# Stores of the squared tiles issued by GpSimd instead of ScalarE, and the last two tiles of each chunk emptied later

## The chip, the cores and the metric

The kernel runs on one core of a Trainium2 chip. Its metric is the device time of one execution in microseconds. A core has engines with a queue of instructions each: TensorE (PE) multiplies matrices, VectorE (DVE) and ScalarE (ACT) work on elements, GpSimd (POOL) and SyncE (SP) here mostly issue DMAs; any of ScalarE, GpSimd and SyncE can issue one. TensorE accumulates in PSUM banks of 128 x 512 numbers.

## The reference

One decoder layer, in float32, on 256 tokens of width 2048:

```
h = RMSNorm(x);  p = h @ W_in
A = dilated sliding-window attention (8 heads);  B = latent attention (8 heads)
x = x + RMSNorm(concat(A, B) @ W_out)
h = RMSNorm(x)
u = square(relu(h @ W_up))        # W_up 2048 x 8192
x = x + RMSNorm(u @ W_down)       # W_down 8192 x 2048
```

The change lies in the line that makes `u`, the up projection. Only float32 accuracy counts as right, so every weight and activation is split into a high part and a low part, and a product is formed from three: high by high, high by low, low by high.

## The kernel before, in words

**Splitting weights.** A tile of weights is loaded to `raw`; ScalarE writes the rounded copy `hi` (L314, or L318 where the norm's gain is multiplied in), and VectorE writes `lo`, the weight less `hi` (L315, L319). TensorE then runs the three products (`three`, L304). So each tile passes through ScalarE, then VectorE, then TensorE.

**The up projection** (the loop over `j`, 0 to 7) makes 1024 columns of `u`, a *chunk*, at a time, over 16 blocks of 128 rows of W_up. Four PSUM banks `acc_u` hold the chunk: 2 halves of the tokens (`b`) by 2 halves of the columns (`n`). Chunk 0 takes its blocks one by one. Chunks 1 to 7 take k6 to k10, then a *pair*, then k11 and k12, a pair, k13, a pair, k14 and k15. A pair (`seven_products`) replaces two blocks by seven smaller products of sums, in the manner of Strassen, and needs both row blocks of weights at once (`seven`): a load of 1 MB into the buffer `ab` or `ab2` (`load_two`, L379), VectorE's sums `t` (L366) and `u` (L370, L371), and four splits, of a corner of `ab`, of `b` (half of `ab`), of `u` and of `t`. GpSimd's queue issues these loads; those of chunk 7's pairs 1 and 2 and chunk 6's pair 2 are loaded as plain tiles by SyncE ("raw" in `UP_PAIRS`), and that of chunk 1's pair 0 by SyncE too. The profile shows both buffers as `ab`; the pairs of a chunk alternate between them, so the next load can be issued as soon as the splits of the pair before the last are done. Pairs are counted 0, 1, 2 in this text. Some of the seven products go to extra banks, `m`, which the previous chunk's `acc_u` have left.

**Emptying a chunk.** When a chunk's products are done, VectorE adds the pairs' combined banks to `acc_u` (L1259, four adds), and each of the four banks is emptied by `up_evac`: ScalarE's Relu with the norm's factor (L1043) and Square (L1044) make a tile `r` (three buffers, shared with the tiles `neg`), which is stored to `rkeep` in DRAM, 256 KB (L1046). Later it is read back in another layout (`turn_u`, `c<-rkeep`, L1059, issued by ScalarE), and VectorE transposes it in blocks of 32 (L1061) into `uT`. For some columns `lo_away` (chunks 1 to 5) then stores the negated rounded tile (`neg`, L1075; `ukeep`, L1077, issued by ScalarE) and adds `uT` to it by an accumulating DMA from GpSimd's queue (`ukeep<-uT`, L1087). The last chunk's squares go straight to `uT` and are stored from there (`rkeep<-uT`).

**What sets the order.** The program is recorded in one pass. `Flow` keeps a clock that each matmul advances by its estimated time; side work is written as generators that yield a delay, and at every `pump` those whose time has come write their next instructions. `up_evac` yields 2.4 (`UP_STEP`) times its `order` before its Relu, in a chunk's own order 0.6, 1.6, 2.6 and 3.6 for its four banks; chunk 0 passes other numbers. The loads and sums of a pair are written when TensorE's weights are taken up to a few tiles before it. Each engine then executes its own instructions in that order, waiting by semaphores.

Of the kernel before, what the change touches and what calls it, by code (L numbers as in the profile page):

```python
# [93 lines left out]
D_X0, D_X, D_SS, D_TAB = 8.0, 3.0, 3.0, (14.0, 20.0)  # L94
D_NORM, D_HT, D_SECOND = 4.5, 1.5, 4.0

UP_STEP = 2.4

D_BACK, D_TURN, D_NEG, D_LO, D_ADD = 12.0, 8.0, 9.0, 2.0, 26.0

# [171 lines left out]
def layer(nc, tc, io):  # L272
    flow = Flow()

    def pool(name, side, **kw):
        return tc.alloc_tile_pool(name=name, bufs=1, side=side, **kw)
# [9 lines left out]
    def bank(i, name):  # L286
        return ps.tile([P, 512], F32, tag=f"bank{i}", bufs=1, name=name)
# [5 lines left out]
    def acc_bank(name):  # L293
        return next_bank(0, 4, name)
# [152 lines left out]
    for c in range(2):  # L447
        wide_d.append([])
        for what, k in DOWN_STEPS[c]:
            if what == "k":  # L450
                ts = [weights.plan(down_weight(c, k), 1, CW)]
            else:
                q, parts_q, back = [lambda c=c, k=k, f=f: f(c, k) for f in (down_sums, down_split, down_back)]
# [4 lines left out]
    def in_order(n, apart=(0, 0)):  # L458

        f, l = apart[0], n - apart[1]  # L460
        return ([(t, b) for b in range(NB) for t in range(f)] + [(t, b) for t in range(f, l) for b in range(NB)]
                + [(t, b) for b in range(NB) for t in range(l, n)])

    def proj(aT, chs, name, order=None, need=None, bank_of=None):

        accs = [[[(bank_of or acc_bank)(f"acc_{name}_{c}_{b}_{i}") for i in range(len(ch.cuts))] for b in range(NB)]
                for c, ch in enumerate(chs)]
        order = order or [(0, t, b) for t, b in in_order(len(chs[0].tiles))]
        left = {(c, b): len(ch.tiles) for c, ch in enumerate(chs) for b in range(NB)}
        uses = {}  # L470
        for c, t, b in order:
            ch = chs[c]
            i, k0, kp = ch.tiles[t]
            ws = [weights.get(x) for x in (i if isinstance(i, list) else [i])]
            i = i if isinstance(i, list) else [i]
            if need:
                need(k0 + kp - 1, b)
            if i[0] < FINE:
                hl = [(0, 0), (1, 0)], [(0, 1)]
            else:  # L480
                hl = [(0, 0), (0, 1), (1, 0)],
            for g, passes in enumerate(hl):
                for kk in range(kp):
                    k = k0 + kk
                    for j, (o, m) in enumerate(ch.cuts):
                        wt, o = (ws[j], 0) if len(ws) > 1 else (ws[0], o)
                        for p, (x, w) in enumerate(passes):
                            mm(accs[c][b][j][:, :m], tok(aT[x], k, b), wt[w][:, kk, o:o + m],
                               k == 0 and g == 0 and p == 0,
                               k == ch.nk - 1 and g == len(hl) - 1 and p == len(passes) - 1, MM * m / 512)  # L490
                    flow.pump()
            left[c, b] -= 1
            for x in i:
                uses[x] = uses.get(x, 0) + 1
                if uses[x] == NB:
                    weights.free(x)
            if not left[c, b]:
                yield c, b, accs[c][b]
# [216 lines left out]
    for half in range(2):  # L715
        qkv = {}
        for nms in (("qk", "v") if not half else "qkv"):
            accs = [acc for _, _, acc in proj(xT, [ch_a[half, nms]], f"{nms}{half}",
                                              bank_of=at_bank if (half, nms) == (0, "v") else None)]
            for i, nm in enumerate(nms):  # L720
                if half and nm == "v":
                    flow.finish(*heads)
                if not half and nm != "v":
                    t = early.tile([P, NB + 1, 512], F32, name=f"{nm}_{half}")
                else:
                    t = pa.tile([P, NB + (nm != "v"), 512], F32, tag=nm, name=f"{nm}_{half}")
# [149 lines left out]
    for what, ch in ch_b:  # L876
        if what == "qr":
            flow.finish(q_chain)
        if what in ("qr", "v0", "v1"):
            if what == "qr":  # L880
                qr = lat.tile([P, NB, HB, RB], F32, tag="cq", name="qr")
            for _, b, acc in proj(latT["q" if what == "qr" else "kv"], [ch], what):
                if what == "qr":
                    out = qr[:, b].rearrange("p h d -> p (h d)")
                else:
                    i = 4 * int(what[1])
                    out = vB[:, b, i:i + 4, :].rearrange("p h d -> p (h d)")
# [3 lines left out]
        else:  # L891
            t, i = qT if what[0] == "q" else kT, 4 * int(what[1])
# [100 lines left out]
    for ns in ((0, 1), (2,), (3,)):  # L993
# [4 lines left out]
        for c, b, acc in proj(mixT, [ch_o[n] for n in ns], f"o{ns[0]}", order, heads_done):  # L998
            n = ns[c]
# [26 lines left out]
    def u_tile(j):  # L1026
        if j not in uT:
            if j in (0, 1, 10, 11, 12, 13):
                t2 = late["u01" if j < 2 else "ab2" if j < 12 else "ab"][:, j % 2 * CW:(j % 2 + 1) * CW]
            else:  # L1030
                tag = {"tag": "T", "bufs": 2} if j > 13 else {"tag": f"uT{j}", "bufs": 1}
                t2 = late["up"].tile([P, CW], F32, name=f"uT{j}", **tag)
            uT[j] = t2.rearrange("p (k s) -> p k s", k=4)
        return uT[j]

    def up_evac(j, b, acc, order):

        yield UP_STEP * order
        if j < GT - 2:
            r = late["up"].tile([P, 512], F32, tag="r", bufs=3, name=f"r{j}_{b}")  # L1040
        else:
            r = u_tile(j)[:, 2 * b:2 * b + 2, :].rearrange("p k s -> p (k s)")
        nc.scalar.activation(r, acc, AF.Relu, scale=rstd2[b])  # L1043
        nc.scalar.activation(r, r, AF.Square)  # L1044
        keep = dram.tile([P, 512], F32, name=f"rkeep{j}_{b}")
        nc.scalar.dma_start(out=keep.rearrange("(a t) (q c) -> (t q) a c", a=4, q=4),  # L1046
                            in_=r.rearrange("m (a c) -> m a c", a=4))
        flow.start(turn_u(j, b, keep), D_BACK + (8.0 if (j, b) == (GT - 1, NB - 1) else 0.0))

# [154 lines left out]
    evac = []  # L1204
    for j in range(FF // CW):
        at = {bn: 4 * (j % 2) + i for i, bn in enumerate(PARTS)}
        if j == 0:
            accs = {bn: acc_bank(f"acc_u0_{bn[0]}{bn[1]}") for bn in at}
            at = {bn: (turn[0] - 3 + i) % 4 for i, bn in enumerate(at)}
        else:  # L1210
            accs = {bn: bank(i, f"acc_u{j}_{bn[0]}{bn[1]}") for bn, i in at.items()}
        steps = wide_u[j]
        order = in_order(len(steps), (APART[1], 0)) if j == 0 else [(t, b) for t, (w, _, _) in enumerate(steps)
                                                                    for b in range(NB if w == "k" else 1)]
        for t, b in order:
            what, k, tiles = steps[t]
            if (j, t, b) == (0, 8, 0):
                flow.finish(*res)
                late["po"].release()
                mix.release()  # L1220
                late["up"] = pool("up", "right")
                late["st"] = late["up"].tile([P, ST], F32R, tag="st", bufs=1, name="st")
                for n in ("ab", "ab2", "c", "u01"):
                    late[n] = late["up"].tile([P, 2 * CW], F32, name=n)
                flow.start(all_sums())
            if (j, t, b) == (FF // CW - 1, 4, 0):
                weights.limit -= 1
                u_next = split_u(0, 0)
            if j == 1 and what == "w":
                flow.until(lambda: len(sums) > k)  # L1230
            if what == "k":
                w = weights.get(tiles[0])
                h_done(k, b)
                for n in range(2):
                    c = slice(n * 512, (n + 1) * 512)
                    three(accs[b, n], [tok(hT[x], k, b) for x in range(2)], [w[x][:, 0, c] for x in range(2)], t == 0, t == len(steps) - 1)
                    if j == 0 and t == len(steps) - 1:
                        evac.append(flow.start(up_evac(n, b, accs[b, n], 0.75 * (2 * b + n))))
                    flow.pump()
                if b == NB - 1:  # L1240
                    weights.free(tiles[0])
                continue

            first, last = k == 0, k == N_SEVEN[j] - 1
            if first:
                weights.ahead = W_AHEAD
                flow.finish(*evac[-4:])
                m = {n: bank(i, f"m{n}_{j}") for n, i in zip((1, 6, 7, 5), free)}
            blocks = [[tok(hT[x], 2 * k + kk, bb) for x in range(2)] for kk, bb in ((0, 0), (1, 0), (1, 1))]
            if last:  # L1250
                weights.ahead -= 1
            seven_products(tiles, (blocks, sums[k]), accs, m, first, last, last and N_SEVEN[j] > 3)
            if last:
                more = close(closing(), m)
        free = [at[bn] for bn in PARTS]
        if j:

            for bn in PARTS:
                nc.vector.tensor_tensor(out=accs[bn], in0=accs[bn], in1=more[bn], op=OP.add)  # L1259
            for o, (b, n) in enumerate(PARTS):  # L1260
                evac.append(flow.start(up_evac(2 * j + n, b, accs[b, n], o + 0.6)))
    weights.ahead = W_AHEAD
    u_last = evac[-4:]
    up = late["up"]
# [88 lines left out]
    for c in range(2):  # L1353
# [3 lines left out]
        accs = {(b, n): y[b][2 * c + n] for b, n in PARTS}  # L1357
# [118 lines left out]
```

## Time and profile before

| | before |
|---|---|
| timed, median of 3 | 1020.69 us (1020.38 to 1021.37) |
| profiled execution | 1022.37 us, span 1020.6 us |
| busy: TensorE | 1009.9 us (99%) |
| busy: VectorE | 841.5 us (82%) |
| busy: ScalarE | 624.8 us (61%) |
| busy: GpSimd | 101.3 us (10%) |
| stores of `rkeep` in the up projection | 28 from `r`, 4 from `uT`, 256 KB each |
| 1 MB loads into `ab` | 17 from GpSimd's queue |

A row of a timeline gives start, duration, engine, line, operation, the tile written and the tiles read, how many such instructions in a row, and in brackets how long the engine stood idle just before and what ended that. "ACTq" and "POOLq" are instructions of those engines' queues that issue a DMA. A row of the waits gives the total, the number of times and the longest. A row of DMA issues gives the number, the KB of each and the median time from issue to landing.

### The profile page before, as it was taken

What the parts mean: (1) busy time and instruction counts of PE and PEld (TensorE: products, weight loads), DVE (VectorE), ACT (ScalarE), POOL (GpSimd) and SP (SyncE); (2) the same over time, 40 slices, a digit from 0 to 9 for tenths busy, and PEclk for the clock granted to TensorE, in tenths of its full rate; (3) what the DMA queues carried; (4) which work ended last, traced back from release to release, by engine and by line L of the source; (5) the groups of instructions that cost most, each with busy time, mean ns of one, the idle gap of its engine ahead of it and who ended that gap; (6) DMA issues with size and microseconds to landing.
All of it is one profiled execution on the core that took longest, in us unless ns stands there. A gap on an engine that the chain in (4) does not pass through costs nothing.

```text
span 1020.6 us, 13297 instructions
## 1 busy us (share of the span) xinstructions
PE 1009.9 (99%) x4670; PEld 842.0 (83%) x4670; DVE 841.5 (82%) x1127; ACT 624.8 (61%) x824; POOL 101.3 (10%) x160
## 2 busy tenths in 40 slices
PE   9999999999999999999999999999999999999996
PEld 6888889898888788888888888888878888888885
DVE  6676747676656779998999989897999999898985
ACT  6585446555463567676666775676666665767661
POOL 0020302102101200000010100000110000211100
PEclk9999999999999999999999999999999999999999
DMA  8977759656687478778988979679989867888952
GB/s 286 367 248 269 244 167 310 220 173 194 199 320 209 174 286 260 245 258 247 293 271 279 284 215 302 190 255 339 346 271 389 292 241 257 296 305 327 368 188 82
DMA packets 109170, 267.07 MB, mean 262 GB/s; under 512 B 9520, under 2 KB 28464, under 8 KB 108464
## 3 DMA queue, kind: packets, MB, share of 16 engines
q1 hardware_dynamic: 65584, 175.14, 50.2%
q0 software_dynamic: 20144, 71.31, 21.1%
q10 hardware_dynamic: 23376, 19.78, 6.2%
q8 instruction: 36, 0.59, 0.2%
q14 instruction: 30, 0.25, 0.1%
HBM read 232.64 MB, written 33.56 MB: 261 GB/s over the span
## 4 chain that ended last, share of the span: by engine, by line
PE 89%; DVE 5%; DMA 2%; issue 2%; ACT 1%; POOL 0%; ACTq 0%; DVEq 0%; POOLq 0%; SPq 0%
PE acc_u L304 26%; PE y L304 19%; PE acc_o L304 8%; PE m L304 6%; PE acc_v L304 5%; PE md L304 5%; PE acc_qk L304 4%; PE acc_q L304 3%; PE acc_k L304 3%; PE acc_ckv L304 3%; DVE lo L315 2%; PE acc_cq L304 2%; DMA rkeep<-uT 1%; PE sc_b L304 1%; DMA raw<-in_w_in 1%
## 5 line engine op out<-in xcount | busy, mean ns | idle before, releaser
L315 DVE TENSOR_TENSOR lo<-raw,hi 128x1024 fp32r<-128x1024 f32 (+2 forms) x205 | 233.4, 1157 | 66.6 <-ACT hi L314 65.4
L314 ACT ACTIVATE hi<-raw 128x1024 fp32r<-128x1024 f32 (+2 forms) x205 | 202.5, 1005 | 75.5 <-DMA raw<-in_w_in 22.8
L304 PE MATMUL acc_u<-hi,hT_lo 128*128 128x512 f32 x386 | 150.3, 389 | 0.5 <-DVE hT_lo L315 0.5
L304 PE MATMUL acc_u<-hi,hT_hi 128*128 128x512 f32 x386 | 150.7, 390 | 0.0
L304 PE MATMUL acc_u<-lo,hT_hi 128*128 128x512 f32 x386 | 150.2, 389 | 0.0
L304 PE MATMUL y<-lo,uhi 128*128 128x512 f32 x358 | 139.4, 389 | 0.4 <-DVE lo L315 0.4
L304 PE MATMUL y<-hi,ulo 128*128 128x512 f32 x358 | 139.4, 389 | 0.1
L304 PE MATMUL y<-hi,uhi 128*128 128x512 f32 x358 | 139.3, 389 | 0.0
L318 ACT ACTIVATE hi<-raw,gcol 128x1024 fp32r<-128x1024 f32 x86 | 96.7, 1148 | 34.2 <-DMA raw<-in_w_up 13.7
L319 DVE SCALAR_TENSOR_TENSOR lo<-raw,gcol,hi 128x1024 fp32r<-128x1024 f32 x86 | 106.6, 1274 | 9.7 <-ACT hi L318 9.6
L304 PEld LDWEIGHTS acc_u<-hi,hT_lo 128*128 128x128 f32 x386 | 72.4, 188 | 16.0 <-DVE hT_lo L315 0.9
L304 PEld LDWEIGHTS acc_u<-hi,hT_hi 128*128 128x128 f32 x386 | 72.5, 188 | 14.9
L304 PEld LDWEIGHTS acc_u<-lo,hT_hi 128*128 128x128 f32 x386 | 72.5, 188 | 14.8
L304 PEld LDWEIGHTS y<-lo,uhi 128*128 128x128 f32 x358 | 67.2, 188 | 14.7 <-DVE lo L315 0.8
L304 PEld LDWEIGHTS y<-hi,ulo 128*128 128x128 f32 x358 | 67.2, 188 | 14.4 <-DVE ulo L315 0.5
L304 PEld LDWEIGHTS y<-hi,uhi 128*128 128x128 f32 x358 | 67.2, 188 | 14.0
L315 DVE TENSOR_TENSOR lo<-st_down,hi 128x1024 fp32r<-128x1024 f32 x46 | 55.0, 1219 | 0.8 <-ACT hi L314 0.8
L304 PE MATMUL acc_o<-hi,mixT_hi 128*128 128x512 f32 x128 | 51.3, 401 | 0.0
L314 ACT ACTIVATE hi<-u 128x1024 fp32r<-128x1024 f32 (+1 forms) x33 | 32.3, 980 | 30.3 <-PE y L304 12.0
L304 PE MATMUL md<-hi,s 128*128 128x512 f32 x138 | 49.9, 389 | 0.0
L304 PE MATMUL acc_o<-hi,mixT_lo 128*128 128x512 f32 x128 | 49.9, 390 | 0.0
L304 PE MATMUL acc_o<-lo,mixT_hi 128*128 128x512 f32 x128 | 49.8, 389 | 0.0
(356 smaller groups left out, 2046.4 us busy)
## 6 DMA issues: line engine op xcount, KB each, us to landing
raw<-in_w_up SPq DMA_DIRECT2D x86, 512.0 KB, 4.9
raw<-in_w_down SPq DMA_DIRECT2D x82, 512.0 KB, 6.3
raw<-in_w_in SPq DMA_DIRECT2D x55, 512.0 KB, 5.6
ab<-in_w_up POOLq DMA_DIRECT2D x17, 1024.0 KB, 6.9
raw<-in_w_out SPq DMA_DIRECT2D x32, 512.0 KB, 4.6
ab_down<-in_w_down POOLq DMA_DIRECT2D x11, 1024.0 KB, 9.3
ulo<-ukeep POOLq DMA_DIRECT2D x20, 512.0 KB, 6.3
rkeep<-r ACTq DMA_DIRECT2D x28, 256.0 KB, 3.6
```

The lines of the kernel that those rows point to most:

```text
L304: nc.tensor.matmul(out, a, b, start=start, stop=stop)
L314: nc.scalar.activation(hi, src, AF.Copy)
L315: nc.vector.tensor_tensor(out=lo, in0=src, in1=hi.bitcast(F32), op=OP.subtract)
L318: nc.scalar.activation(hi, src, AF.Copy, scale=g)
L319: nc.vector.scalar_tensor_tensor(out=lo, in0=src, scalar=g, in1=hi.bitcast(F32), op0=OP.mult, op1=OP.subtract)
```

## The change

The store of each squared tile is issued by GpSimd instead of ScalarE, all 32 of them. In chunks 1 to 7 the third and the fourth emptying are put later in the recorded order: 3.4 and 4.2 steps of 2.4 instead of 2.6 and 3.6. Chunk 0's emptying keeps its own order.

```
-UP_STEP = 2.4
+UP_STEP, EVAC = 2.4, (0.6, 1.6, 3.4, 4.2)
...
         nc.scalar.activation(r, acc, AF.Relu, scale=rstd2[b])
         nc.scalar.activation(r, r, AF.Square)
         keep = dram.tile([P, 512], F32, name=f"rkeep{j}_{b}")
-        nc.scalar.dma_start(out=keep.rearrange("(a t) (q c) -> (t q) a c", a=4, q=4),
+        nc.gpsimd.dma_start(out=keep.rearrange("(a t) (q c) -> (t q) a c", a=4, q=4),
                             in_=r.rearrange("m (a c) -> m a c", a=4))
...
             for o, (b, n) in enumerate(PARTS):
-                evac.append(flow.start(up_evac(2 * j + n, b, accs[b, n], o + 0.6)))
+                evac.append(flow.start(up_evac(2 * j + n, b, accs[b, n], EVAC[o])))
```

GpSimd's instructions around the start of chunk 5, before. `ab_3458` and `ab` are the two buffers: the first load of `ab_3458` here is chunk 5's pair 1, the `ab` after it chunk 5's pair 2, and the next `ab_3458` chunk 6's pair 0.

```order
L379 DMA ab<-in_w_up 128x2x1024
L1087 DMA ukeep_4704<-uT_4584 128x512
L379 DMA ab_3458<-in_w_up 128x2x1024
L379 DMA ab<-in_w_up 128x2x1024
L1087 DMA ukeep_5069<-uT_4949 128x512
L379 DMA ab_3458<-in_w_up 128x2x1024
```

The same place after the change:

```order
L379 DMA ab<-in_w_up 128x2x1024
L1087 DMA ukeep_4722<-uT_4584 128x512 x2
L1046 DMA rkeep_0_5099<-r_0_5096 128x4x128
L1046 DMA rkeep_0_5123<-r_0_5120 128x4x128
L1046 DMA rkeep_1_5160<-r_1_5157 128x4x128
L379 DMA ab_3458<-in_w_up 128x2x1024
L1046 DMA rkeep_1_5186<-r_1_5183 128x4x128
L379 DMA ab<-in_w_up 128x2x1024
L379 DMA ab_3458<-in_w_up 128x2x1024
```

Three of the four stores now stand ahead of the load for pair 1 and the fourth ahead of the load for pair 2. It is the same at the starts of chunks 2, 3, 4 and 6. At the start of chunk 1 all four stand ahead of pair 1's load.

ScalarE at the same place, from the split of the first pair's `u`, before (`acc_u_10` and `acc_u_11` are the third and the fourth bank of chunk 4):

```order
L314 ACTIVATE hi_5131<-u_0_5103 128x1024
L1043 ACTIVATE r_1_5144<-acc_u_10_4713,rstd_pre_3394 128x512
L1044 ACTIVATE r_1_5144<-r_1_5144 128x512
L1046 DMA rkeep_1_5147<-r_1_5144 128x4x128
L314 ACTIVATE hi_5152<-t_0_5102 128x1024
L1043 ACTIVATE r_1_5165<-acc_u_11_4714,rstd_pre_3394 128x512
L1044 ACTIVATE r_1_5165<-r_1_5165 128x512
L1046 DMA rkeep_1_5168<-r_1_5165 128x4x128
L318 ACTIVATE hi_5181<-raw_5179,gcol 128x1024
L318 ACTIVATE hi_5203<-raw_5201,gcol 128x1024
```

After:

```order
L314 ACTIVATE hi_5130<-u_0_5103 128x1024
L1077 DMA ukeep_5087<-neg_1_5128 128x512
L314 ACTIVATE hi_5147<-t_0_5102 128x1024
L1043 ACTIVATE r_1_5157<-acc_u_10_4710,rstd_pre_3394 128x512
L1044 ACTIVATE r_1_5157<-r_1_5157 128x512
L318 ACTIVATE hi_5176<-raw_5174,gcol 128x1024
L1043 ACTIVATE r_1_5183<-acc_u_11_4711,rstd_pre_3394 128x512
L1044 ACTIVATE r_1_5183<-r_1_5183 128x512
L318 ACTIVATE hi_5203<-raw_5201,gcol 128x1024
```

The split of `t` now precedes the third emptying, and the split of block k11 precedes the fourth. VectorE's instructions keep their order here but for the transposes. After the change, from the split of the first pair's `t` (`t_1` and `u_1` are the sums of pair 1, the two `raw` are k11 and k12):

```order
L315 TENSOR_TENSOR lo_5148<-t_0_5102,hi_5147 128x1024
L366 TENSOR_TENSOR t_1_5169<-ab_3458 128x1024
L370 TENSOR_TENSOR u_1_5170<-t_1_5169,ab_3458 128x512
L371 TENSOR_TENSOR u_1_5170<-u_1_5170,ab_3458 128x512
L319 SCALAR_TENSOR_TENSOR lo_5177<-raw_5174,gcol,hi_5176 128x1024
L319 SCALAR_TENSOR_TENSOR lo_5204<-raw_5201,gcol,hi_5203 128x1024
```

The sums of pair 1 stand ahead of the low parts of k11 and k12, as they did before. TensorE's and SyncE's orders are the same in both kernels.

More of the change, by code (lines that the diff above doesn't have):

```diff
@@ L95 @@
 D_NORM, D_HT, D_SECOND = 4.5, 1.5, 4.0
-UP_STEP = 2.4
+UP_STEP, EVAC = 2.4, (0.6, 1.6, 3.4, 4.2)
 D_BACK, D_TURN, D_NEG, D_LO, D_ADD = 12.0, 8.0, 9.0, 2.0, 26.0
@@ L1045, in up_evac @@
         keep = dram.tile([P, 512], F32, name=f"rkeep{j}_{b}")
-        nc.scalar.dma_start(out=keep.rearrange("(a t) (q c) -> (t q) a c", a=4, q=4),
+        nc.gpsimd.dma_start(out=keep.rearrange("(a t) (q c) -> (t q) a c", a=4, q=4),
                             in_=r.rearrange("m (a c) -> m a c", a=4))
@@ L1260, in layer @@
             for o, (b, n) in enumerate(PARTS):
-                evac.append(flow.start(up_evac(2 * j + n, b, accs[b, n], o + 0.6)))
+                evac.append(flow.start(up_evac(2 * j + n, b, accs[b, n], EVAC[o])))
     weights.ahead = W_AHEAD
```

## The prediction

> **What bounds the kernel now.** I read the page's totals first, then busy times cut into stretches of the up projection, then the waits, then each engine's timeline at a chunk boundary. The totals, and one chunk period plus the change to the down projection (columns: stretch, TensorE, weight loads, VectorE, ScalarE, GpSimd busy, granted clock, DMA share, GB/s):
>
> ```profile
> span 1020.6 us, 13297 instructions
> PE 1009.9 (99%) x4670; PEld 842.0 (83%) x4670; DVE 841.5 (82%) x1127; ACT 624.8 (61%) x824; POOL 101.3 (10%) x160
> ...
> 554.00:596.00 42.00, 42.00 (x187) 34.79 (x186) 39.35 (x45) 28.67 (x34) 4.02 (x5) 1.00 0.89 276
> 596.00:637.00 41.00, 41.00 (x183) 33.95 (x182) 38.26 (x43) 28.56 (x33) 2.50 (x3) 1.00 0.80 253
> ...
> 710.00:755.00 45.00, 44.57 (x196) 36.26 (x195) 44.31 (x57) 29.23 (x34) 5.58 (x8) 1.00 0.95 336
> ```
>
> TensorE sets the time: in the chunks it is busy in every microsecond, at clock 1.00. Relief of another engine can therefore gain only what TensorE lacks, 0.43 us in the last stretch. But VectorE is close behind: 39.35 of 42 us, 2.65 us free. ScalarE has 13 us free.
>
> How near VectorE follows, shown by the chain of waits (TensorE begins k11 of chunks 5 and 6) and by VectorE making chunk 6's low parts of k11 and k12:
>
> ```profile
> 571.38 1.36 PE m L304 x6
> 572.74 5.44 PE acc_u L304 x24
> ...
> 614.22 5.44 PE acc_u L304 x24
> ```
>
> ```profile
> 606.78 1.22 DVE L366 TENSOR_TENSOR t<-ab 128x1024 f32<-128x1024 f32 x1
> ...
> 609.37 2.47 DVE L319 SCALAR_TENSOR_TENSOR lo<-raw,gcol,hi 128x1024 fp32r<-128x1024 f32 x2
> ```
>
> The first low part is done at 609.37 + 2.47/2 = 610.6, and TensorE starts k11 at 614.2: a lead of 3.6 us. A VectorE delay beyond that reaches TensorE. Ahead of these low parts in VectorE's queue stands t<-ab, the first of pair 1's sums; it reads the 1 MB that GpSimd's queue loads. So the question is how early that load is issued. GpSimd's timeline, and its waits:
>
> ```profile
> 394.20 0.72 POOL L379 DMA_DIRECT2D ab<-in_w_up  x1 [29.81 <-DVE lo L315]
> ...
> 538.13 0.71 POOL L379 DMA_DIRECT2D ab<-in_w_up  x1 [6.16 <-DVE lo L315]
> 560.65 0.71 POOL L379 DMA_DIRECT2D ab<-in_w_up  x1 [21.80 <-DVE lo L315]
> 561.36 0.96 POOL L1087 DMA_DIRECT2D ukeep<-uT  x1
> ...
> POOL ab L379 <- DVE lo L315: 216.4, 16, 29.8
> ```
>
> GpSimd waits for free buffers and little else: its queue runs ahead. Chunk 5's pair 1 is loaded by the issue at 538.13, and VectorE reads it at 564.95 (below), 26.8 us later. The row at 561.36 also shows that an instruction behind a waiting load goes out only after it: the queue keeps its order.
>
> **The change part by part.** The edits act at the chunk boundary. VectorE there in chunk 5, from the first add of the old chunk's sums:
>
> ```profile
> 553.55 2.48 DVE L1259 TENSOR_TENSOR acc_u<-acc_u,c 128x512 f32<-128x512 f32 x4
> ...
> 561.07 1.23 DVE L315 TENSOR_TENSOR lo<-u,hi 128x1024 fp32r<-128x1024 f32 x1 [0.72 <-ACT hi L314]
> 563.81 1.23 DVE L315 TENSOR_TENSOR lo<-t,hi 128x1024 fp32r<-128x1024 f32 x1 [1.51 <-ACT hi L314]
> 564.95 1.22 DVE L366 TENSOR_TENSOR t<-ab 128x1024 f32<-128x1024 f32 x1
> ...
> 567.54 2.48 DVE L319 SCALAR_TENSOR_TENSOR lo<-raw,gcol,hi 128x1024 fp32r<-128x1024 f32 x2
> ```
>
> ScalarE there:
>
> ```profile
> 555.66 0.38 ACTq L1046 DMA_DIRECT2D rkeep<-r  x1
> ...
> 559.98 1.06 ACT L314 ACTIVATE hi<-u 128x1024 fp32r<-128x1024 f32 x1 [1.07 <-PE acc_u L304]
> 560.94 0.67 ACT L1043 ACTIVATE r<-acc_u,rstd_pre 128x512 f32<-128x512 f32 x1
> 561.64 0.63 ACT L1044 ACTIVATE r<-r 128x512 f32<-128x512 f32 x1
> ...
> 562.72 1.06 ACT L314 ACTIVATE hi<-t 128x1024 fp32r<-128x1024 f32 x1 [0.44 <-PE acc_u L304]
> 563.68 0.67 ACT L1043 ACTIVATE r<-acc_u,rstd_pre 128x512 f32<-128x512 f32 x1
> 564.38 0.63 ACT L1044 ACTIVATE r<-r 128x512 f32<-128x512 f32 x1
> ```
>
> What is taken away: 32 store issues on ScalarE at 0.38 us, 12 us over the up projection. It also moves hi<-t ahead of the third emptying, so VectorE's 1.51 us wait for it shrinks. On an engine 13 us free per chunk, ahead of an always busy TensorE, both are worth nothing, at most the 0.43 us.
>
> What is added: 32 store issues on GpSimd, each waiting for a Square of ScalarE. By order, pair 1's load now stands behind the third store of the same boundary (chunks 2 to 6), or behind all four (chunk 1). It can no longer go out 27 us early; it goes out after that Square. Chunk 7 loads pair 1 on SyncE and has no such load.
>
> The cost in chunk 5, from A = 553.55:
> 1. Third Square done. Before: 561.64 + 0.63 = A + 8.7. Now hi<-t (1.06) comes first, and three store issues (1.1) and their gaps fall away, but the third Relu cannot follow hi<-t earlier than u and the second negation allow. I place it at A + 9.4, 0.7 later; bounds A + 7.5 (everything ahead moves up by the issues saved) and A + 11.
> 2. The third store's issue on GpSimd. No row has this store there; neighbours are
>
> ```profile
> L1087 POOL DMA_DIRECT2D ukeep<-uT x8 | 7.5, 933 | 15.8 <-DVE acc_u L1259 15.8
> ...
> L974 POOL DMA_DIRECT2D xkeep<-x x8 | 4.3, 541 | 8.1 <-DVE hT_lo L315 6.9 <-DVE x L958 1.2
> ```
>
> both 256 KB. I take 0.93, as ukeep comes from the same place in the program; 0.54 is the other bound.
> 3. Landing of the 1 MB, counted from its issue. The median row of these loads, and then the fastest, the slowest, and the one at this very place of chunk 5 (issued 413.69, 572.05, 560.65; minimum, median, maximum of a single load):
>
> ```profile
> ab<-in_w_up POOLq DMA_DIRECT2D x17, 1024.0 KB, 6.9
> ...
> DMA to landing us min/median/max: 5.2/5.2/5.2
> ...
> DMA to landing us min/median/max: 8.9/8.9/8.9
> ...
> DMA to landing us min/median/max: 6.0/6.0/6.0
> ```
>
> I take 6.5: the 6.0 of this place plus 0.5 for the store's 256 KB directly ahead. Bounds 5.2 and 8.9.
> 4. So t<-ab starts at A + 9.4 + 0.9 + 6.5 + about 0.1 of wake-up = A + 17.0, against 564.95 − A = 11.4: **5.6 us late**, with VectorE idle and the low parts of k11 and k12 stuck behind it. VectorE cannot make it up: of its 2.65 us free per period, 0.72 + 1.51 lie before this sum, so 0.4 are left after it, and each such chunk adds its own 5.6. Chunks 2 to 6 (chunk 2 without the negations, which I neglect): 5 × 5.6 = 28.0.
>
> Chunk 1, where the load waits for the fourth Square:
>
> ```profile
> 396.49 0.63 ACT L1044 ACTIVATE r<-r 128x512 f32<-128x512 f32 x1
> ...
> 397.16 1.22 DVE L366 TENSOR_TENSOR t<-ab 128x1024 f32<-128x1024 f32 x1
> ```
>
> Three earlier store issues fall away, 1.1 us, of which I credit 0.9: Square done at 396.2, + 0.9 + 6.5 + 0.1 = 403.7, 6.6 late. VectorE's small gaps there give back 0.8: 5.8.
>
> VectorE is then 28.0 + 5.8 = 33.8 us late at chunk 6's k11. TensorE had 3.6 of lead, used up once: **30.2 us**. In chunk 7 the lead is smaller:
>
> ```profile
> 653.73 2.47 DVE L319 SCALAR_TENSOR_TENSOR lo<-raw,gcol,hi 128x1024 fp32r<-128x1024 f32 x2
> ...
> 655.70 5.44 PE acc_u L304 x24
> ```
>
> 655.70 − (653.73 + 1.24) = 0.7, so 2.9 more of the delay would show, but VectorE regains some 2.4 of it there (1.5 on the wait for the u part, the rest on earlier issues); +0.5. The down projection returns the 0.43 us. Sum: 30.2 + 0.5 − 0.4 = 30.3.
>
> Costs taken as nothing. The later third and fourth emptying: the first pair takes those two banks with the six m matmuls at 571.38, A + 17.8, and the fourth emptying should end by A + 12.5; the read-backs stay on ScalarE behind work already queued; if one came late, VectorE's transpose would wait, at the few microseconds a landing takes. Pair 2's load, now behind the fourth store, goes out at about A + 13 and lands by A + 22; before, VectorE read it at A + 20.4 (row below), now 5.6 later, A + 26: hidden by the stall itself. Without the stall it would be the next to be late.
>
> ```profile
> 573.94 1.22 DVE L366 TENSOR_TENSOR t<-ab 128x1024 f32<-128x1024 f32 x1
> ```
>
> The profiled execution took 1022.37 us around its 1020.6 us span, so the changed one should take 1052.7; the timed median of before lies 1.7 lower, at 1020.69, which gives 1051.0.
>
> A rule that adds to this: TensorE would stand still about 5.6 us in each chunk, and its granted clock in this trace has 1.00 throughout, with no such stop. The Trainium skill, in "TensorE: Matmul & The Clock Gate" (Part 1), says that an idle window of about 3.4 us halves the clock until as long a busy window has passed; by it each stall would cost some 1.7 us more of TensorE, an estimate from that page. As VectorE leads the pace by then, only the last would show, and the sum would be 1052.7. No row here tests it, and I leave it out.
>
> **The rivals.**
>
> *Heavier, 0.10.* The third Relu writes a buffer of which there are three, so it may also wait for the first store's landing. That store is issued at about A + 2.1, and lands 3.6 us on by ScalarE's queue, 7.3 by the nearest row of GpSimd's:
>
> ```profile
> rkeep<-r ACTq DMA_DIRECT2D x28, 256.0 KB, 3.6
> ...
> ukeep<-uT POOLq DMA_DIRECT2D x8, 256.0 KB, 7.3
> ```
>
> At 7.3 with 0.93 of issue the Relu starts at A + 10.3 instead of A + 8.1, 2.2 more per chunk in five chunks, 11; with landings of 8.9 for the loads, 2.4 × 6 = 14 more. Either gives 1062 to 1065, both 1076. Against it: ukeep<-uT reads and writes its target, these stores only write.
>
> *Lighter, 0.06.* ScalarE, freed of the issues, is at the third Square by A + 7.5, the issue takes 0.54, the landing 5.2: t<-ab at A + 13.3, 1.9 late. Six times that, less the 3.6, is 8 us: 1029.
>
> *Not slower, 0.07.* The loads are not held up by the stores, and TensorE stays full: 1020.3, with the 0.43 us regained. For it: a load issued 26.8 us ahead of its use could go out some 20 us later unnoticed. Against it: the order of GpSimd's instructions and the row at 561.36. The Trainium skill speaks for it, in "DMA: Bandwidth & Descriptors" (Issuing engines are not separate DMA queues): which engine issues a DMA saves or costs only its sequencer's time, little beside the transfer. The same page (Anatomy of one DMA) has semaphore waits happen on the issuing sequencer, before dispatch, and the trace agrees with that: 561.36 follows 560.65. By the first rule alone the time would be 1020.7.
>
> **How the numbers follow.** Forecast 0.77, heavier 0.10, lighter 0.06, not slower 0.07. The forecast's own bounds: landings of 5.2 in all six chunks take off 8 and ScalarE at its early bound 5 × 1.9 = 9.5, together 1034; landings of 8.9 add 14, 1065. The range 1034 to 1067 leaves out the two light cases and part of the heavy one, 0.18. A measurement of this kernel tells about 0.2% (2 us) from no change. Faster 0.02 and same 0.05 come from the case without delay; slower 0.93 is all the rest.
>
> **What would show it.** In the changed profile: VectorE idle 4 to 8 us before t<-ab of pair 1 in chunks 1 to 6, ended by the load of ab; TensorE idle about 1 to 3 us at k11 of chunk 1 and 5 to 6 in chunks 2 to 6, none in chunk 7; a chunk period of about 47 us instead of 41.5; GpSimd's loads released by ScalarE's Square (L1044) instead of VectorE's lo; the third store's issue near 0.9 us. I would be wrong if pair 1's loads still went out long before the Square, if VectorE stopped for less than 2 us per boundary, or if TensorE idled first at another place, such as the fourth emptying's banks or a late read-back.

## The result and the profile after

The changed kernel takes 1050.93 us (median of 4, 1050.11 to 1051.26) against 1020.58 us: a ratio of 1.0295, 95% interval 1.0279 to 1.0311, so 30 us slower. Its profiled execution took 1051.26 us, with a span of 1049.5 us, 28.9 more than before. One execution of a kernel below (two stores on GpSimd) took 5564 us against 1021 to 1024 for its other nine, and is left out of its median. The page's totals, and then busy times by chunk (columns as in the prediction):

```profile
span 1049.5 us, 13328 instructions
PE 1018.5 (97%) x4670; PEld 847.1 (81%) x4670; DVE 841.2 (80%) x1127; ACT 620.6 (59%) x824; POOL 125.7 (12%) x192
```

```profile
401.00:445.00 44.00, 44.00 (x195) 36.10 (x194) 39.07 (x43) 26.78 (x31) 4.38 (x6) 1.00 0.62 205
445.00:492.00 47.00, 42.80 (x183) 34.96 (x182) 39.07 (x43) 27.87 (x34) 5.16 (x8) 0.96 0.70 234
...
587.00:634.00 47.00, 43.38 (x184) 35.40 (x183) 39.06 (x43) 27.90 (x34) 6.99 (x10) 0.96 0.77 246
634.00:680.00 46.00, 42.24 (x179) 34.45 (x178) 39.77 (x45) 27.02 (x32) 5.63 (x7) 0.96 0.76 247
```

VectorE does about the same work per chunk as before (39.06 us), but a chunk now lasts some 47 us. TensorE has holes from chunk 2 on, and its granted clock is 0.96 there. GpSimd's timeline at the start of chunk 5, and VectorE's (the old chunk's add starts at A = 574.78):

```profile
577.15 0.79 POOL L1046 DMA_DIRECT2D rkeep<-r  x1 [22.05 <-ACT r L1044]
579.34 0.78 POOL L1046 DMA_DIRECT2D rkeep<-r  x1 [1.40 <-ACT r L1044]
584.60 0.75 POOL L1046 DMA_DIRECT2D rkeep<-r  x1 [4.48 <-ACT r L1044]
585.34 0.72 POOL L379 DMA_DIRECT2D ab<-in_w_up  x1
586.88 0.79 POOL L1046 DMA_DIRECT2D rkeep<-r  x1 [0.81 <-ACT r L1044]
```

```profile
574.78 2.49 DVE L1259 TENSOR_TENSOR acc_u<-acc_u,c 128x512 f32<-128x512 f32 x4
...
583.30 1.22 DVE L315 TENSOR_TENSOR lo<-t,hi 128x1024 fp32r<-128x1024 f32 x1
591.41 1.23 DVE L366 TENSOR_TENSOR t<-ab 128x1024 f32<-128x1024 f32 x1 [6.90 <-DMA ab<-in_w_up]
...
594.01 2.47 DVE L319 SCALAR_TENSOR_TENSOR lo<-raw,gcol,hi 128x1024 fp32r<-128x1024 f32 x2
```

The load of pair 1 follows the third store without a gap at 585.34; before the change it was issued 15 us before the add, now 10.6 us after it. VectorE stands idle for 6.90 us until it lands. The waits count six such stops, one per chunk from 1 to 6; and of TensorE, five:

```profile
DVE t L366 <- DMA ab<-in_w_up: 42.3, 6, 7.5
```

```profile
PE acc_u L304 <- DVE lo L319: 20.4, 5, 5.2
```

TensorE's timeline behind one of them (chunk 5, k11) shows where the rest went:

```profile
595.34 0.50 PE L304 MATMUL acc_u<-lo,hT_hi 128*128 128x512 f32 x1 [3.62 <-DVE lo L319]
...
596.58 0.63 PE L304 MATMUL acc_u<-hi,hT_lo 128*128 128x512 f32 x1
597.01 0.63 PE L304 MATMUL acc_u<-hi,hT_hi 128*128 128x512 f32 x1
597.43 0.63 PE L304 MATMUL acc_u<-lo,hT_hi 128*128 128x512 f32 x1
...
599.79 0.40 PE L304 MATMUL acc_u<-lo,hT_hi 128*128 128x512 f32 x1
600.02 0.39 PE L304 MATMUL acc_u<-hi,hT_lo 128*128 128x512 f32 x1
```

For 3.4 us (596.15 to 599.55) the matmuls start 0.43 us apart instead of 0.23. TensorE's busy time grew by 8.6 us (1009.9 to 1018.5) with the same 4670 matmuls: some 1.7 us behind each of the five stops. The 20.4 us of stops and these 8.6 are 29.0, the whole 28.9 of the span.

### The profile page after: what moved, and what is told of

It reads as the page before. It is cut to its first block, busy times and chain, and to the rows that moved or that the text cites. A ratio compares the mean times of both kernels' runs of the same rounds, so it can differ in the third digit from the quotient of the medians.

```text
span 1049.5 us, 13328 instructions
## 1 busy us (share of the span) xinstructions
PE 1018.5 (97%) x4670; PEld 847.1 (81%) x4670; DVE 841.2 (80%) x1127; ACT 620.6 (59%) x824; POOL 125.7 (12%) x192
## 4 chain that ended last, share of the span: by engine, by line
PE 78%; issue 9%; DVE 5%; DMA 4%; ACT 2%; POOL 1%; SPq 0%; DVEq 0%; POOLq 0%; ACTq 0%
PE y L304 25%; PE acc_u L304 13%; PE acc_o L304 8%; PE md L304 6%; PE acc_v L304 5%; PE acc_qk L304 4%; DMA ab<-in_w_up 3%; PE acc_q L304 3%; PE acc_k L304 3%; PE m L304 3%; PE acc_ckv L304 2%; DVE lo L319 2%; PE acc_cq L304 2%; PE sc_b L304 1%; POOL rkeep L1046 1%
## 5 line engine op out<-in xcount | busy, mean ns | idle before, releaser
L304 PE MATMUL acc_u<-lo,hT_hi 128*128 128x512 f32 x386 | 154.6, 400 | 20.4 <-DVE lo L319 20.4
L304 PE MATMUL acc_u<-hi,hT_lo 128*128 128x512 f32 x386 | 153.5, 398 | 0.4 <-DVE hT_lo L315 0.4
L304 PE MATMUL acc_u<-hi,hT_hi 128*128 128x512 f32 x386 | 153.5, 398 | 0.0
L304 PEld LDWEIGHTS acc_u<-hi,hT_lo 128*128 128x128 f32 x386 | 74.6, 193 | 16.6 <-DVE hT_lo L315 0.9
L366 DVE TENSOR_TENSOR t<-ab 128x1024 f32<-128x1024 f32 x18 | 22.0, 1221 | 42.3 <-DMA ab<-in_w_up 42.3
```

The source lines that it names most:

```text
L304: nc.tensor.matmul(out, a, b, start=start, stop=stop)
L366: tt(out=two[0], in0=two[1][:, 0:2, :], in1=two[1][:, 1:4:2, :], op=OP.add)
```

## The experiments

**The stores alone, and the order alone.** Each half of the change by itself.

```
e1:  EVAC = (0.6, 1.6, 2.6, 3.6)          # stores on GpSimd, old order
e2:  nc.scalar.dma_start(out=keep...)     # stores on ScalarE, new order
```

> The stores go to GpSimd, the emptying keeps its old order. All four stores of a boundary then stand ahead of pair 1's load in chunks 1 to 6. Theory (the load waits behind the last Square ahead of it in GpSimd's queue): the fourth Square should end about 1.1 us later than the third one does in the changed kernel, so the load lands about 1 us later in chunks 2 to 6: 1054 to 1058 us, a little slower than the changed kernel. Rival (the later third and fourth emptying is what costs): most of the loss is gone, under 1030 us. Rival (a store on GpSimd's queue costs as such): like the changed kernel, 1051 us.

Measured: 1055.83 us, ratio 1.0336 (1.0320 to 1.0351). As the queue's order says: four stores ahead of the load cost more than three. The later emptying is not the cause; with the stores on GpSimd it spares about 5 us. In chunk 5 of this kernel pair 1's load goes out 11.3 us after the add instead of 10.6, and takes 7.1 us to land instead of 6.0.

> The third and fourth emptying are later, the stores stay on ScalarE. Theory: TensorE stays full, no load waits: 1020 to 1021 us, and VectorE's wait of 1.5 us for the split of t is gone. Rival (the later emptying costs): some 1025 to 1050 us.

Measured: 1020.66 us, ratio 0.9995 (0.9986 to 1.0005). VectorE's wait for the split of `t` is gone in this profile, and with TensorE always busy that brings nothing.

**The loads first.** All 32 stores stay on GpSimd; a pair's load (`fetch`) is recorded eight weight tiles earlier, in one kernel for pair 1 only, in another for pairs 1 and 2.

```
-        for n, f in (*more, (0, fetch), (-late_sums, sums), ...
+        for n, f in (*more, (early, fetch), (-late_sums, sums), ...
...
e3:  early=8 if k == 1 and UP_PAIRS[j][1] != 'raw' else 0
e8:  early=8 if k and UP_PAIRS[j][k] != 'raw' else 0
```

> The changed kernel with one difference: pair 1's load is recorded eight weight tiles earlier, so that it stands ahead of all four stores in GpSimd's queue; all 32 stores stay on GpSimd, all emptyings late. Theory: the load goes out early again, VectorE does not wait for it, and the time is that of the kernel before: 1020 to 1022 us; pair 2's load, behind the fourth store, should land around 19 us after VectorE's first add and be just in time. Rival (stores on GpSimd cost as such, by their issue or their traffic): still 1030 to 1050 us.

Measured: 1027.56 us, ratio 1.0063 (1.0048 to 1.0078). Most of the loss is gone, but 6.4 us stay, more than expected. Its VectorE still waits for loads, in four chunks (two rows; line numbers are one or two higher in this kernel):

```profile
493.42 1.23 DVE L367 TENSOR_TENSOR t<-ab 128x1024 f32<-128x1024 f32 x1 [3.76 <-DMA ab<-in_w_up]
...
583.35 1.23 DVE L367 TENSOR_TENSOR t<-ab 128x1024 f32<-128x1024 f32 x1 [5.23 <-DMA ab<-in_w_up]
```

These are the sums of pair 2, whose load stands behind the fourth store. Behind the second of them TensorE comes to its one stop, of 3.77 us. GpSimd issued that load here:

```profile
571.50 0.76 POOL L1048 DMA_DIRECT2D rkeep<-r  x1 [1.53 <-ACT r L1046]
572.25 0.71 POOL L380 DMA_DIRECT2D ab<-in_w_up  x1
```

From 572.25 to 583.35 are 11.1 us; the loads for these four sums took 8.5 to 11.0 us to land, where I had counted 6 to 6.5. Whether these loads are the rest was put to a test:

> The changed kernel with the loads of pairs 1 and 2 recorded eight weight tiles earlier: pair 1's stands ahead of all four stores, pair 2's behind the second and ahead of the third. All 32 stores stay on GpSimd, all emptyings late. Theory (what the kernel with pair 1's load first still loses is pair 2's load behind the fourth store): VectorE waits for no load and the time is 1020 to 1021.5 us. Rival (stores on GpSimd's queue still cost something, as the 6 us of that kernel): 1025 to 1028 us.

Measured: 1020.72 us, ratio 0.9997 (0.9988 to 1.0006). VectorE waits for no load in the up projection, and nothing is left of the loss, with every store on GpSimd and every emptying late. At the start of chunk 5 its GpSimd shows (lines one or two higher):

```profile
557.48 0.79 POOL L1048 DMA_DIRECT2D rkeep<-r  x1 [15.83 <-ACT r L1046]
559.66 0.78 POOL L1048 DMA_DIRECT2D rkeep<-r  x1 [1.39 <-ACT r L1046]
562.19 0.71 POOL L380 DMA_DIRECT2D ab<-in_w_up  x1 [1.75 <-DVE lo L316]
564.40 0.77 POOL L1048 DMA_DIRECT2D rkeep<-r  x1 [1.50 <-ACT r L1046]
566.68 0.76 POOL L1048 DMA_DIRECT2D rkeep<-r  x1 [1.50 <-ACT r L1046]
```

So a store on GpSimd's queue has no price of its own here; what stands behind it has.

**Fewer stores ahead of the load.** Two ways to leave only two stores ahead of pair 1's load: the third and fourth emptied so late that they fall behind it, or stored by ScalarE.

```
e6:  EVAC = (0.6, 1.6, 4.2, 5.0)
e4:  (nc.scalar if b else nc.gpsimd).dma_start(out=keep...)
```

> All 32 stores on GpSimd, third and fourth emptying still later (4.2 and 5.0 steps), so that only the first two stores stand ahead of pair 1's load in chunks 2 to 6 and the last two ahead of pair 2's. Theory: pair 1's load goes out about 5.3 us after VectorE's first add and lands at about 11.4, where the sum began before the change; pair 2's lands at about 19.6 against 20.4 wanted. Chunk 1 keeps all four stores ahead of the load, or three, and costs up to 5 us of VectorE's time, of which TensorE's lead hides 3.6. So 1020 to 1023 us. Rival (the later the emptying, the slower): over 1051 us.

Measured: 1029.65 us, ratio 1.0086 (1.0069 to 1.0102): the direction of the theory, but 7 us more than its upper end. The load, in chunk 4 (add at 517.51):

```profile
523.11 0.78 POOL L1046 DMA_DIRECT2D rkeep<-r  x1 [2.44 <-ACT r L1044]
523.88 0.71 POOL L379 DMA_DIRECT2D ab<-in_w_up  x1
```

```profile
517.51 2.49 DVE L1259 TENSOR_TENSOR acc_u<-acc_u,c 128x512 f32<-128x512 f32 x4
...
530.91 1.23 DVE L366 TENSOR_TENSOR t<-ab 128x1024 f32<-128x1024 f32 x1 [3.86 <-DMA ab<-in_w_up]
```

The recorded order also puts the first negation ahead of the second emptying, which the expectation left out, so the load goes out 6.4 us after the add instead of 5.3, and takes 7.0. The sum of pair 1 starts at A + 13.4, 2.0 late. Chunk 2, without negations, adds no delay; with 3.9 from chunk 1 and about 2 from each of chunks 3 to 6, less the lead of 3.6, some 8 are due, and 8.8 were measured.

> The changed kernel, but the third and fourth store of each chunk are issued by ScalarE again; the first two stay on GpSimd. Pair 1's load then waits for the second Square only, is issued about 5.3 us after VectorE's first add and lands 6 to 7 us later, at 11.4 to 12.5; VectorE read it at 11.4 before the change. Theory: 0 to 1 us late per chunk, mostly within TensorE's lead of 3.6 us: 1020.3 to 1023 us. Rival (each store on GpSimd costs alike): half the loss, 1035 us.

Measured: 1023.23 us, ratio 1.0020 (1.0010 to 1.0029), just above the expected stretch's end. TensorE stops twice in its profile, for 1.25 and 1.15 us. Half the stores on GpSimd cost about 2 us, far from half the loss.

**The last chunk.** Only its four stores on GpSimd, in the kernel before.

```
+        (nc.gpsimd if j >= GT - 2 else nc.scalar).dma_start(out=keep...)
```

> The kernel before, with only the last chunk's four stores (straight from the tiles of u) on GpSimd; no load stands behind them in the up projection. Theory: ScalarE's wait of 5.1 us for one of these stores may shrink, but TensorE lacked only about 0.5 us there: 1020.0 to 1020.7 us. Rival (that wait mattered): 1016 to 1019 us.

Measured: 1021.15 us, ratio 1.0000 (0.9991 to 1.0009): no gain that can be told.

**TensorE's lead.** Stores on GpSimd for chunk 0 alone (one load held up), or for chunks 0 and 1 (two loads), the rest on ScalarE, in the new order.

```
e9:   (nc.gpsimd if j < 2 else nc.scalar).dma_start(out=keep...)
e10:  (nc.gpsimd if j < 4 else nc.scalar).dma_start(out=keep...)
```

> The changed kernel, but only chunk 0's four stores go to GpSimd, the others stay on ScalarE. Only chunk 1's load of pair 1 is then held up; VectorE is some 4 to 5 us late once. Theory (TensorE's lead of 3.6 us is used up once and hides that much): 1020.5 to 1022 us. Rival (a late load costs its full lateness at once): 1025 us.

Measured: 1021.19 us, ratio 1.0005 (0.9996 to 1.0014). VectorE waited 7.10 us for the load and the end did not move:

```profile
402.24 1.23 DVE L366 TENSOR_TENSOR t<-ab 128x1024 f32<-128x1024 f32 x1 [7.10 <-DMA ab<-in_w_up]
432.56 2.49 DVE L1259 TENSOR_TENSOR acc_u<-acc_u,c 128x512 f32<-128x512 f32 x4
472.67 2.49 DVE L1259 TENSOR_TENSOR acc_u<-acc_u,c 128x512 f32<-128x512 f32 x4
```

The adds of the kernel before, for comparison:

```profile
428.54 2.48 DVE L1259 TENSOR_TENSOR acc_u<-acc_u,c 128x512 f32<-128x512 f32 x4
...
470.13 2.48 DVE L1259 TENSOR_TENSOR acc_u<-acc_u,c 128x512 f32<-128x512 f32 x4
...
637.04 2.48 DVE L1259 TENSOR_TENSOR acc_u<-acc_u,c 128x512 f32<-128x512 f32 x4
```

So the next add is 4.0 us late, and the one after it 2.5. The lead took the delay, and VectorE began to make it up. But the lead is larger here than the 3.6 us that I had counted, which is that of chunk 6. In the kernel before, VectorE's first low part of k11 and, from the chain of waits, TensorE's start of k11, in chunk 1:

```profile
399.75 2.47 DVE L319 SCALAR_TENSOR_TENSOR lo<-raw,gcol,hi 128x1024 fp32r<-128x1024 f32 x2
...
406.82 5.44 PE acc_u L304 x24
```

The low part is done at 401.0 and TensorE takes it at 406.8, 5.8 us later. The sum of pair 1 is 5.1 us late in this kernel (402.24 against 397.16), within that lead.

> The changed kernel with the stores of chunks 0 and 1 alone on GpSimd: two loads held up, in chunks 1 and 2. Theory: VectorE is about 9 us late after the second, TensorE's lead hides 3.6, and TensorE stops at k11 of chunk 2 for some 4 us as in the changed kernel; with 1.7 us of half clock behind it, this time not followed by another stop that absorbs it: 1024.5 to 1027 us. Rival (no lead, full lateness): 1030 us. Rival (each load costs the sixth part of the loss): 1031 us.

Measured: 1029.38 us, ratio 1.0078 (1.0065 to 1.0091), the five times between 1027.1 and 1030.7. The second load brings TensorE to a stop of 4.26 us in chunk 2, the only one. The loss is above what I expected and near the 1030 and 1031 us of the rivals. But VectorE's sum is 9.1 us late in chunk 2 (448.36 against 439.28) and TensorE stops for less than half of that, so there is a lead. The profiled execution, 1027.09 us, is 6.2 above the median of before: the stop and 1.7 us of slow matmuls behind it make 6.0.

**The half clock.** The changed kernel with 18 matmuls of zeros ahead of k11 in chunks 2 to 6, and the kernel with two loads held up, with them in chunk 2 only. They add zero to the accumulators and fill the stop.

```
+                if k == 11 and b == 0 and 1 < j < 7:      # e11: j == 2
+                    for i in range(18):
+                        nc.tensor.matmul(accs[PARTS[i % 4]], nought[:, :P], nought, start=False, stop=False)
```

> The changed kernel with 18 matmuls of zeros added to the accumulators ahead of k11 in chunks 2 to 6, about 4 us of TensorE's work that fills most of each stop; the result does not change by them. It tells what the half clock after each stop is worth: TensorE's busy time grew by 8.6 us with the change. Theory (VectorE's lateness sets the pace, so the slow matmuls are hidden by TensorE's lead in all chunks but the last): granted clock 1.00 in those chunks, and 1049 to 1050 us, 1 to 2 us less than the changed kernel. Rival (the slow matmuls are part of the loss): 1042 us. Rival (the added matmuls delay k11 themselves): 1055 us and more.

Measured: 1051.45 us, ratio 1.0296 (1.0282 to 1.0310). The clock is 1.00 in all these chunks, and the time does not change. The slow matmuls were no part of the loss that could be won back: VectorE's lateness sets the pace, and in their absence TensorE stops again where VectorE is late (9.0 us in six stops). The 1 to 2 us that I expected at the end did not appear.

> The stores of chunks 0 and 1 alone on GpSimd, and 18 matmuls of zeros ahead of k11 in chunk 2, where TensorE stopped for 4.3 us and then ran 9 or so matmuls at half pace. The added work fits the stop. No later stop can absorb the slow stretch in this pair of kernels, so its price must show: theory, 1.5 to 2 us less than the same kernel without the zeros (measured beside it). Rival (VectorE is late in any case and the slow stretch is free, as it seemed with all six loads held up): the same within 0.5 us.

> The kernel with the stores of chunks 0 and 1 alone on GpSimd, once more as the partner of the run with zeros, and since its times lay apart (1027.1 to 1030.7 us): 1027 to 1030 us again. If they lie apart again, the loss in this kernel depends on something that differs between executions, such as the landing time of the two loads.

Measured: with the zeros 1025.92 us, ratio 1.0055 (1.0043 to 1.0068); without, 1028.23 us, ratio 1.0072 (1.0059 to 1.0086). The point values differ by 2.3 us in the way of the theory, but the intervals overlap by a little. The ten executions without zeros, of both runs, took 1027.1 to 1030.7 us, the five with them 1025.6 to 1028.1. Of the two profiles without zeros, the stretch around the stop shows a different clock:

```profile
445.00:492.00 47.00, 42.74 (x182) 34.87 (x181) 42.50 (x47) 27.57 (x33) 2.21 (x4) 0.96 0.81 275
```

```profile
445.00:492.00 47.00, 42.39 (x177) 34.51 (x176) 42.08 (x47) 27.38 (x32) 2.19 (x4) 0.93 0.80 274
```

The first is the earlier run, profiled at 1027.09 us, the second the repeat, at 1028.23 us. The stops are nearly the same (4.26 and 4.61 us), but the clock is at half for 3.4 us in the first and 6.8 us in the second, there from 451.1 on, while TensorE still stood. Counted over the time in which TensorE was busy, the slow clock cost 1.7 and 2.6 us. With the stops that is 6.0 and 7.3 us, and the two times lie 1.1 apart. Of the ten executions, the three below 1027.2 us have a mean granted clock of 0.996 or 0.997, and six of the other seven 0.994. That this makes the whole scatter was not shown.

## Why the prediction was right, point by point

The time, 1050.93 us against 1051.0, came out closer than its steps deserve. The sum was 30.3 us and the span grew by 28.9; the step from the profiled execution to the median, taken as 1.7 us less, was only 0.3 less for the changed kernel (1051.26 and 1050.93), and this made up for it, by luck.

- **The cause held.** GpSimd's queue keeps its order, the load waits for the Square, VectorE for the load, TensorE for VectorE. The kernel with both loads ahead, which alone undoes the order and keeps the stores and the late emptying, has no loss.
- **The third Square** was put at A + 9.4: in chunk 5 it ends at 584.31, A + 9.5, and the store's issue starts 0.3 behind it. In chunk 4 the store came 1.0 later, at A + 10.8 (537.05, add at 526.22). What differs is the second negation's wait for the landing of the first one's store; ScalarE in chunk 4, and in chunk 5:

```profile
532.99 0.63 ACT L1075 ACTIVATE neg<-uT 128x512 fp32r<-128x512 f32 x1 [2.50 <-DMA ukeep<-neg]
...
580.54 0.63 ACT L1075 ACTIVATE neg<-uT 128x512 fp32r<-128x512 f32 x1 [1.49 <-DMA ukeep<-neg]
...
583.67 0.64 ACT L1044 ACTIVATE r<-r 128x512 f32<-128x512 f32 x1
```

- **The store's issue** was put at 0.93 us and took 0.75 to 0.79; the **landing** at 6.5 and was 6.0 or 6.1 in five chunks and 6.6 in chunk 4. The bounds were far wider than needed.
- **Each chunk's delay** was put at 5.6. The adds lie 4.2, 9.2, 14.4, 21.2, 26.5 and 31.8 us later than before in chunks 2 to 7, so chunks 2 to 6 added 5.0, 5.2, 6.9, 5.2 and 5.3, in all 27.6 against 28.0. The 6.9 of chunk 4 is the later store (1.0) and the longer landing (0.6). Chunk 1 was put at 5.8 and gave 4.2: the first step that failed, mis-sized by 1.6. The store behind its fourth Square went out at 395.58, where the sum had the Square done at 396.2 only; issue and landing took 0.75 and 6.0 instead of 0.93 and 6.5. So the sum of pair 1 was 5.3 late (402.42 against 397.16) instead of 6.6, and VectorE gave back 1.1 instead of 0.8.

```profile
432.74 2.49 DVE L1259 TENSOR_TENSOR acc_u<-acc_u,c 128x512 f32<-128x512 f32 x4
...
479.32 2.49 DVE L1259 TENSOR_TENSOR acc_u<-acc_u,c 128x512 f32<-128x512 f32 x4
...
526.22 2.49 DVE L1259 TENSOR_TENSOR acc_u<-acc_u,c 128x512 f32<-128x512 f32 x4
...
621.73 2.49 DVE L1259 TENSOR_TENSOR acc_u<-acc_u,c 128x512 f32<-128x512 f32 x4
...
668.81 2.49 DVE L1259 TENSOR_TENSOR acc_u<-acc_u,c 128x512 f32<-128x512 f32 x4
```

- **The lead**, 3.6 us used up once, held for chunk 6: VectorE's sum is 31.8 late there (638.55 against 606.78), and TensorE began k11 at 642.48, 28.3 later than before, against the 30.2 of the sum. In chunk 1 the lead is 5.8, so the single load held up, which cost nothing that can be told (ratio 1.0005), tested that a lead hides a delay, and not its size of 3.6.
- **The stops** of TensorE were put at 1 to 3 us in chunk 1 and 5 to 6 behind it. There was none in chunk 1, whose lead of 5.8 the 5.3 us of lateness did not use up, and 3.6 to 5.2 in the others. The half clock is what was missing: each slow stretch uses up 1.7 us of TensorE's lead, and the next stop is shorter by as much. The delays that chunks 3 to 6 added, less 1.7, are 3.5, 5.2, 3.5 and 3.6; the stops there are 3.6, 5.2, 3.6 and 3.8.
- **The half clock** was left out of the sum. The Trainium skill, in "TensorE: Matmul & The Clock Gate" (Part 1), says that an idle window of about 3.4 us halves the clock until a busy one has passed, and the trace of the changed kernel agrees: stops of 3.6 to 5.2 us, and a clock at half for 3.4 us each time. Another run does not: in the kernel with the third and fourth emptying still later, TensorE stopped for 1.90 us in chunk 5 and then ran 3.4 us at half clock as well, while a stop of 1.91 us in its chunk 4, and one of 2.20 us in the changed kernel with zeros, had no such stretch. How long a stop must be is thus not settled here.

```profile
578.52 0.50 PE L304 MATMUL acc_u<-lo,hT_hi 128*128 128x512 f32 x1 [1.90 <-DVE lo L319]
...
580.76 0.63 PE L304 MATMUL acc_u<-lo,hT_hi 128*128 128x512 f32 x1
```

With all six loads held up, filling the stops with zeros left the time where it was. With two it was faster by 2.3 us, with overlapping intervals. Between the start of k11 in chunk 6 (28.3 late) and in chunk 7 (685.64 against 655.70, 29.9 late) TensorE did lose 1.7, where the sum had 0.5; why the changed kernel with zeros does not gain that is open, but its load of chunk 6 let VectorE begin 0.8 later (639.4 against 638.55), and TensorE stopped 0.55 us in chunk 7.
- **The end.** From k11 of chunk 7 on 1.0 us was regained, not 0.4.
- **Pair 2's load** was called hidden by the stall, and next to be late without it. The kernel with pair 1's load first shows exactly that, at 8.5 to 11.0 us of landing.
- **The heavier, lighter and not-slower rivals** fell. The third Relu was held up by the negation's store, not by `rkeep`, whose stores landed in 3.3 us from GpSimd's queue and not in 7.3. That the issuing engine matters little, the ground of the not-slower rival, holds here for the stores themselves (ratio 0.9997 with all 32 on GpSimd), not for the loads behind them.

```profile
rkeep<-r POOLq DMA_DIRECT2D x28, 256.0 KB, 3.3
```

## What to carry to other kernels

Moving the waiting stores to another engine's queue cost nothing by itself here; the price was paid by the loads that stood behind them there. Before moving one, list what the queue issues ahead of time (here loads 27 us early), and keep those loads ahead of anything that waits for fresh results. Relief of an engine that is not the bound, 12 us of ScalarE here, brought nothing by itself.

## What was not expected of the hardware

- The landing of a 1 MB load differs by its place: 6.0 to 6.6 us for pair 1's in the changed kernel, 8.5 to 11.0 for pair 2's in chunks 2 to 5 of the kernel with pair 1's load first. The traffic of the core does not explain it: in the 11.0 us the DMA share was 0.73, in the 6.0 us of chunk 5 in the changed kernel 0.85. The cause stays open.
- Behind a stop TensorE's granted clock was at half for 3.4 us in each of the five stops of the changed kernel, some 8 matmuls at 0.43 us each. It was 6.8 us, a part of it before TensorE began again, behind three of the five stops with the stores moved alone, and behind the one stop of two other executions (pair 1's load first; two loads held up, the second run). What decides between the two was not shown.
